# RWKV-7 branch beside sparse attention on one core: the RWKV step laid out anew, attention loads issued a unit ahead

## The chip, the cores and the metric

One core of a Trainium2 chip. Its engines each work through a queue of their own: TensorE (PE; PEld is its weight loads), VectorE (DVE), ScalarE (ACT), GpSimd (POOL) and SyncE (SP), whose queue issues the DMA transfers. The metric is the device time of one execution in microseconds, the median of the runs. PEclk in the profile is the TensorE clock that was granted, as a share of its upper level of 2.4 GHz; its lower level is 1.2 GHz.

## The reference

One layer over 2048 tokens, width 1024, all in float32: RMS norm, a projection into everything that follows, two branches, an output projection with residual, a final norm.

- **RWKV branch**, 8 heads of 64. Per token, state S (64x64 a head): `S = S*w_t + (S·(-kk_t))(kk_t*a_t)^T + v_t k_t^T`, `y_t = S r_t`. Then group norm over the 64 of each head, the bonus `sum(r*k*r_k)*v`, and a gate.
- **Sparse attention branch**, 8 heads: an index score per pair of query and key selects the 256 best keys of a query; softmax attention over those alone; an up-projection per head; a gate.

```
S   = S * w_t + sa * (kk_t * a_t) + v_t * k_t        # sa = S @ (-kk_t), 2048 steps
y_t = S @ r_t
y   = groupnorm(y) * gn_g + gn_b + sum(r * k * r_k) * v
out = rmsnorm(x + concat(y_rwkv * silu(g), o_attn * silu(g2)) @ w_out)
```

## The kernel before, in words

Four phases follow one another in the program text, and share the engines where their data allow. `phase_as` projects, builds the inputs of both branches in DRAM and the top-k masks (to about 986 us). `phase_r` is the RWKV branch, `phase_t` the attention, `phase_w` the output projection, whose first matmul is at 1917 us. RWKV and attention run side by side from 986 to 1917 us.

**RWKV.** The 2048 tokens are cut into 16 chunks of 128, a chunk into two halves (o = 0, 1) of 64 tokens. A chunk has two units (i = 0, 1), each with four of the eight heads. A unit is prepared (`prep`): one load `ld` of its five inputs (L938, two buffers), the running sum of the log decays by a scan on DVE (L951), exponentials on ACT, products into BK and X, and the products of all pairs of tokens on PE (L975) which DVE masks into E (L978). The bonus goes over `ld` once more: products on DVE, a matmul with ones (L983), times v (L985). `systems` sends the diagonal 32x32 blocks of E through DRAM (`du`, L1016) into the table A (L1018, one buffer). `inverse` inverts them on POOL: 31 steps of a multiplication (L1032) and an addition (L1034), each on the one before; the result goes out to `dx` (L1035) and comes back as the table TT (L1039). `prep2` transposes BK and v. `chain` is the recurrence of one half: reads of the state (L1052, L1059), a solve with TT on the first 32 tokens and on the other 32 (L1068), the new state (L1093, added on DVE at L1096), the outputs y. `tail` is the norm of a finished chunk's y, with a power on POOL in the middle (`rpow`, L130), then transposes of y on PE (L1115), scale, bonus, gate and store. In round n of the main loop: both units of chunk n+2 are prepared, chunk n+1 is inverted and transposed, the diagonal blocks of n+2 are sent, chunk n-1 gets its tail, and then both halves of the chain of chunk n run. All but the chain is traced under `later()`.

**Attention.** 64 units (p, b): four pairs of heads, 16 blocks of 128 queries. `scores` takes up to four matrices of 512 keys: two matmuls (L1240, L1241, a split into a high and a low part), evacuated with mask and running maximum by DVE into `sc`, `mx` (L1242), then the exponential on ACT. `attend` of the unit before transposes the weights (L1274), multiplies by v (L1283), gates with `ga` (L1296) and stores (L1297). The two take turns, 512 keys at a time. A unit's mask (L1224), queries (L1217), keys (L1205), values (L1207) and gates (L1265) are loaded by the unit itself when it comes to them.

**What sets the order.** A scheduler places every instruction in the queue of its engine by a planned time, taking the ready one of the highest priority; `later()` lowers the priority of what it encloses by one step, and all of attention stands two steps lower, so that it fills what RWKV leaves free. `issue_after(x)` makes what it encloses queue behind x on x's engine alone; it waits for nothing. Within a queue an instruction that waits holds all that stand behind it.

Of the kernel before, what the change touches and what calls it, by code (L numbers as in the profile page):

```python
# [7 lines left out]
F32 = mybir.dt.float32  # L8
# [10 lines left out]
T = 2048  # L19
# [868 lines left out]
def phase_r(env):  # L888
# [5 lines left out]
    C = 64  # L894
# [37 lines left out]
    def prep(tq, i, eC):  # L932
# [23 lines left out]
        G.tensor_copy(u.eC, eL[:, :, C])  # L956
# [3 lines left out]
        G.tensor_tensor(bp, kk, a, op=OP.mult)  # L960
# [5 lines left out]
        G.tensor_tensor(bp, bp, L, op=OP.mult)  # L966
# [55 lines left out]
    def inverse(A):  # L1022
# [7 lines left out]
        for s in range(31):  # L1030
            m, w = s // 4 + 1, 31 - s
            G.tensor_tensor(tmp[:, :m, :w], Xr[:, :m, s:s + 1].to_broadcast([128, m, w]),  # L1032
                            A[:, s:s + 1, s + 1:].to_broadcast([128, m, w]), op=OP.mult)
            G.tensor_tensor(Xr[:, :m, s + 1:], Xr[:, :m, s + 1:], tmp[:, :m, :w], op=OP.add)  # L1034
# [5 lines left out]
        return TT  # L1040

    def chain(us, TT, eC, y, n, o):
# [5 lines left out]
        def read(plane, pr):  # L1048
# [46 lines left out]
        for h in range(2):  # L1095
            V.tensor_tensor(S1[HALF[h], :, :, h], pS[HALF[h]], SP[HALF[h]], op=OP.add)  # L1096
        S.activation(y[:, o::2], read(1, pst([128, 2, 128], "rp", 2)), AF.Copy)

    def tail(us, y):
# [11 lines left out]
        rpow(st[:, 2], st[:, 1])  # L1111
        V.tensor_tensor(yv, yv, bc(st[:, 2]), op=OP.mult)
        pt = pst([128, NC, 2, C], "ch", 1)
# [19 lines left out]
    def prepare(n):  # L1133

        if n >= N:
            return None
        eC = tl([128, 2, NC], F32, "eC", 4)
        us = [prep(n, i, eC) for i in range(2)]
        return NS(dict(us=us, eC=eC))

    def prepare2(b, after=None):

        if b is None:
            return
        with tc.issue_after(after) if after else ExitStack():
            b.TT = inverse(b.A)
        for u in b.us:
            prep2(u)

    with e.later():  # L1150
        batch = {0: prepare(0)}
        batch[0].A = systems(batch[0].us)
        batch[1] = prepare(1)
        prepare2(batch[0])
        batch[1].A = systems(batch[1].us)
    tails = []
    for n in range(N):
        b = batch.pop(n)
        with e.later():
            batch[n + 2] = prepare(n + 2)  # L1160
            nx = batch.get(n + 1)
            prepare2(nx, batch[n + 2].us[1].last if batch[n + 2] else None)
            if batch[n + 2]:
                batch[n + 2].A = systems(batch[n + 2].us)
            if tails:
                tail(*tails.pop())
        y = tl([128, NC, 128], F32, "y", 2)
        for o in range(2):
            chain(b.us, b.TT, b.eC, y, n, o)
        tails.append((b.us, y))  # L1170
    with e.later():
        tail(*tails.pop())


def phase_t(env):
# [21 lines left out]
    KT, VT, Q = {}, {}, {}  # L1197

    def chunk_in(p, c):
# [10 lines left out]
    def queries_in(p, c):  # L1210

        Q[p, c] = []
        for i in range(2):
            q = tl([128, 2, 256], F32R, f"q{i}", 2)
            for h in range(2):
                for s in range(2):
                    dma(f32(q)[HALF[s], h], e.d_q[i][HALF[h], p, c * 256:c * 256 + 256])  # L1217
            Q[p, c].append(q)

    def scores(p, b, out):  # L1220

        n = (b + 1) * 128
        mk = tl([128, T], BF16, "mk", 3)
        dma(mk[:, :n], e.d_mask[b])  # L1224
        if b % 2 == 0:
            queries_in(p, b // 2)
# [5 lines left out]
        for nt, c0 in enumerate(range(0, n, C)):  # L1232
            w = min(C, n - c0)
            wp = max(w, 256)
            if (p, nt) not in KT:
                chunk_in(p, nt)
# [15 lines left out]
    def attend(p, b, rows, sums):  # L1252
# [11 lines left out]
        ga = tl([128, 128], F32, "ga", 3)  # L1264
        dma(ga, e.d_ga[p][:, ts])  # L1265
# [31 lines left out]
        dma(e.d_y[:, 4 + p, ts], ga)  # L1297

    units = [(p, b) for p in range(NP) for b in range(NB)]
    last = None  # L1300
    for u in units + [None]:
        out = []
        parts = [scores(*u, out)] if u else []
# [4 lines left out]
        last = (*u, *out) if u else None  # L1308

# [74 lines left out]
```

## Time and profile before

| | |
|---|---|
| median of 3 runs | 2110.79 us (2103.02, 2110.79, 2117.44) |
| the profiled execution | 2117.66 us, its span 2115.9 us |
| mean granted clock | 0.906 |
| busy: PE, DVE, ACT, POOL | 1815.5, 1290.4, 1018.7, 866.3 us |

The rows below are of that one execution. Times are in us from the span's start; Lnnn is a line of the kernel before. In a wait, the name behind the arrow is the instruction or transfer that came last of those waited for. A busy time is the sum over the instructions of an engine, so that a stretch less its busy time is idle.

### The profile page before, as it was taken

What the parts mean: (1) busy time and instruction counts of PE and PEld (TensorE: products, weight loads), DVE (VectorE), ACT (ScalarE), POOL (GpSimd) and SP (SyncE); (2) the same over time, 40 slices, a digit from 0 to 9 for tenths busy, and PEclk for the clock granted to TensorE, in tenths of its full rate; (3) what the DMA queues carried; (4) which work ended last, traced back from release to release, by engine and by line L of the source; (5) the groups of instructions that cost most, each with busy time, mean ns of one, the idle gap of its engine ahead of it and who ended that gap; (6) DMA issues with size and microseconds to landing.
All of it is one profiled execution on the core that took longest, in us unless ns stands there. A gap on an engine that the chain in (4) does not pass through costs nothing.

```text
span 2115.9 us, 36553 instructions
## 1 busy us (share of the span) xinstructions
PE 1815.5 (86%) x12906; PEld 1442.2 (68%) x12906; DVE 1290.4 (61%) x2986; ACT 1018.7 (48%) x1934; POOL 866.3 (41%) x2052
## 2 busy tenths in 40 slices
PE   5788998879796989896888877898889888978998
PEld 4666877658575867675667665777677766756886
DVE  5532538979788788986745555555656466524332
ACT  4422495453534754331355554556565655653321
POOL 1110224352545355553545445535655556441100
PEclk9778999989798999997589998999999999988999
DMA  7536334332262434224554354434543543224443
GB/s 247 197 100 202 98 105 135 105 108 88 69 236 63 137 119 140 80 92 132 148 140 111 105 150 112 113 84 111 151 116 100 143 135 103 75 62 165 130 145 111
DMA packets 311602, 262.53 MB, mean 124 GB/s; under 512 B 85105, under 2 KB 260849, under 8 KB 310257
## 3 DMA queue, kind: packets, MB, share of 16 engines
q1 hardware_dynamic: 307024, 248.04, 39.2%
q0 software_dynamic: 4384, 12.06, 1.8%
q8 instruction: 104, 1.70, 0.3%
q14 instruction: 90, 0.73, 0.1%
HBM read 166.37 MB, written 97.85 MB: 125 GB/s over the span
## 4 chain that ended last, share of the span: by engine, by line
PE 35%; DMA 10%; DVE 6%; POOL 4%; issue 2%; ACT 2%; SPq 1%; POOLq 0%; DVEq 0%; ACTq 0%
PE om L1283 5%; DMA ld<-d_rw 5%; PE tr L1274 5%; PE s L1240 3%; PE po L1345 3%; PE po L1346 3%; PE po L1348 3%; PE s L1241 2%; PE rp L975 2%; DMA dx<-Xr 2%; PE ch L1068 1%; DMA q<-d_q 1%; PE ch L1052 1%; PE rp L1059 1%; PE ch L1093 1%
## 5 line engine op out<-in xcount | busy, mean ns | idle before, releaser
L578 PE MATMUL pm<-xh,wh 128*128 128x512 f32 x800 | 330.4, 414 | 19.9 <-DVE t L589 11.8
L579 PE MATMUL pm<-xl,wh 128*128 128x512 f32 x800 | 328.0, 410 | 0.0
L580 PE MATMUL pm<-xh,wl 128*128 128x512 f32 x800 | 326.6, 408 | 0.0
L1242 DVE CUSTOM_DVE_ANT_0 sc<-s,mk 128x512 f32<-128x512 f32 (+3 forms) x320 | 187.5, 606 | 111.1 <-PE s L1241 62.4
L1276 ACT ACTIVATE pt<-tr 128x512 f32<-128x512 f32 (+1 forms) x288 | 157.5, 570 | 107.9 <-PE tr L1274 69.5
L578 PEld LDWEIGHTS pm<-xh,wh 128*128 128x128 f32 x800 | 158.4, 198 | 61.3 <-DVE t L589 13.7
L1240 PE MATMUL s<-kt,q 128*128 128x512 f32 (+2 forms) x320 | 149.7, 470 | 45.1 <-DVE mx L1242 29.3
L580 PEld LDWEIGHTS pm<-xh,wl 128*128 128x128 f32 x800 | 158.0, 197 | 36.3
L579 PEld LDWEIGHTS pm<-xl,wh 128*128 128x128 f32 x800 | 158.0, 198 | 35.5
L1274 PE MATMUL tr<-ident,sc 128*128 128x128 f32 x1088 | 179.1, 291 | 1.0 <-ACT pt L1276 0.9
L1249 ACT ACTIVATE sc<-sc,mx 128x128 f32<-128x128 f32 (+15 forms) x128 | 153.1, 1198 | 43.5 <-DVE mx L1248 42.8
L1283 PE MATMUL om<-pt,vt 128*64 128x128 f32 x2176 | 168.3, 290 | 0.8 <-DVE ga L1266 0.8
L1034 POOL TENSOR_TENSOR Xr<-Xr,Xtmp 128x60 f32<-128x60 f32 (+24 forms) x496 | 151.4, 305 | 34.2
L1032 POOL TENSOR_TENSOR Xtmp<-Xr,A 128x60 f32<-128x60 f32 (+24 forms) x496 | 146.5, 295 | 43.0 <-DMA A<-du 8.7
L1274 PEld LDWEIGHTS tr<-ident,sc 128*128 128x128 f32 x1088 | 132.9, 148 | 30.2 <-issue 12.5
L1283 PEld LDWEIGHTS om<-pt,vt 128*64 128x64 f32 x2176 | 129.9, 143 | 29.6 <-issue 15.6
L318 ACT ACTIVATE mk<-x,st 128x1920 bf16<-128x1920 f16 (+5 forms) x72 | 98.0, 1361 | 103.3 <-POOL st L315 103.3
L250 ACT ACTIVATE rl<-lg,wi 128x512 f32<-128x512 f32 (+3 forms) x152 | 93.9, 631 | 100.6 <-PE lg L248 51.8
L1241 PE MATMUL s<-kt,q 128*128 128x512 f32 (+2 forms) x320 | 125.5, 394 | 8.6 <-DMA q<-d_q 8.5
L321 DVE TENSOR_SCALAR_CACHE_REDUCE mk<-x,st 128x2048 bf16<-128x2048 f16 (+5 forms) x72 | 120.6, 1675 | 1.4
L1240 PEld LDWEIGHTS s<-kt,q 128*128 128x128 f32 x320 | 65.0, 203 | 70.2 <-DVE mx L1242 35.2
L255 DVE SCALAR_TENSOR_TENSOR xs<-rl,wi,xs 128x512 f32<-128x512 f32 (+3 forms) x108 | 73.5, 680 | 60.8 <-ACT rl L250 60.0
(329 smaller groups left out, 3975.1 us busy)
## 6 DMA issues: line engine op xcount, KB each, us to landing
wraw<-in_w_in_dram SPq DMA_DIRECT2D x42, 512.0 KB
d_rw<-t SPq DMA_DIRECT2D x80, 256.0 KB
ld<-d_rw SPq DMA_DIRECT2D x32, 640.0 KB
q<-d_q SPq DMA_DIRECT2D x256, 64.0 KB
d_q<-t SPq DMA_DIRECT2D x32, 256.0 KB
d_kt<-t SPq DMA_DIRECT2D x32, 256.0 KB
kt<-d_kt SPq DMA_DIRECT2D x64, 128.0 KB
A<-du SPq DMA_DIRECT2D x16, 512.0 KB
```

What stands on the lines that cost most here:

```text
L578: PE.matmul(pm, wh[:, k], XH[g][:, k], start=k == 0, stop=False)
L579: PE.matmul(pm, wh[:, k], XL[g][:, k], start=False, stop=False)
L580: PE.matmul(pm, wl[:, k], XH[g][:, k], start=False, stop=k == KD - 1)
L1032: G.tensor_tensor(tmp[:, :m, :w], Xr[:, :m, s:s + 1].to_broadcast([128, m, w]), A[:, s:s + 1, s + 1:].to_broadcast([128, m, w]), op=OP.mult)
L1034: G.tensor_tensor(Xr[:, :m, s + 1:], Xr[:, :m, s + 1:], tmp[:, :m, :w], op=OP.add)
L1240: PE.matmul(pS[:, :wp], qh[:, h, qs], k[:, h, :wp], start=True, stop=False)
L1241: PE.matmul(pS[:, :wp], ql[:, h, qs], k[:, h, :wp], start=False, stop=True)
L1242: V.tensor_tensor_reduce(out=rows[h][:, c0:c0 + w], in0=pS[:, :w], in1=mk[:, c0:c0 + w], scale=1.0, scalar=LOW, op0=OP.add, op1=OP.max, ac ...
L1249: S.activation(rows[h][:, :n], rows[h][:, :n], AF.Exp, bias=mx[:, h, 4:5], accum_out=sums[:, h:h + 1])
L1274: PE.transpose(pt[:, i, h], rows[h][:, (kb + i) * 128:(kb + i) * 128 + 128], ident)
L1276: S.activation(w[:, :m], pt[:, :m], AF.Copy)
L1283: PE.matmul(po[HALF[h]], v[:, (kb + i) % 4, HALF[h]], w[:, i, h], start=kb + i == 0, stop=kb + i == b)
```

## The change

The diff's first part is in `prep` and what it feeds. Two multiplications of a unit (`bp`) go from POOL to DVE, the copy of `eC` from POOL to ACT. The scaling of BK by eC queues on POOL behind an instruction that is handed in: the last step of an inverse. SV is no longer zeroed; the matmuls that read its missing half in the first read now contract over 64 rows instead of 128. `tail` becomes `tail_norm` and `tail_out`, `chain` returns its state addition on DVE, `inverse` its last step.

The main loop is written anew. Round n: the norm of chunk n-1, its power on POOL; the inverse of chunk n+1, queued on POOL behind that power; unit 0 of chunk n+2, its DVE rows queued behind the state addition of the half before; the chain's first half; the transposes and output of chunk n-1; `prep2` of chunk n+1; unit 1 of chunk n+2, queued behind the first half's state addition; the diagonal blocks of n+2; the chain's second half.

In attention `load` issues everything a unit needs, the gates too (`ga` has 5 buffers, before 3), one unit ahead of its scores; a store is issued behind the loads of a later unit; two DMA issues for the two heads of a key or query tile become one.

```
 prep:
-        G.tensor_copy(u.eC, eL[:, :, C])
+        S.activation(u.eC, eL[:, :, C], AF.Copy)
-        G.tensor_tensor(bp, kk, a, op=OP.mult)
+        V.tensor_tensor(bp, kk, a, op=OP.mult)
-        G.tensor_tensor(bp, bp, L, op=OP.mult)
+        V.tensor_tensor(bp, bp, L, op=OP.mult)
-        u.last = G.tensor_tensor(bk, bk, u.eC[:, :, None].to_broadcast([128, NC, 2 * C]), op=OP.mult).ins
+        with tc.issue_after(scaled_after):
+            G.tensor_tensor(bk, bk, u.eC[:, :, None].to_broadcast([128, NC, 2 * C]), op=OP.mult)
 prep2:
-        G.memset(u.SV[HALF[u.i]], 0.0)
 chain, read:
-                m = PE.matmul(pr[HALF[i], g, HALF[h]], us[i].E[:, h, 2 * g + o, plane * C:plane * C + C],
-                              us[i].SV[:, 2 * g + o, HALF[h]], start=False, stop=True, skip_group_check=True)
+                rows = slice(0, 128) if plane else HALF[1 - i]
+                m = PE.matmul(pr[HALF[i], g, HALF[h]], us[i].E[rows, h, 2 * g + o, plane * C:plane * C + C],
+                              us[i].SV[rows, 2 * g + o, HALF[h]], start=False, stop=True, skip_group_check=True)
 main loop (the old one is in the listing above):
+    batch = {}
+    first = G.memset(eLs[0][:, :, 0:1], 1.0).ins
     with e.later():
+        for n in range(2):
+            batch[n] = b = begin(n)
+            for i in range(2):
+                b.us.append(prep(n, i, b.eC, first))
+            b.A = systems(b.us)
+            if n == 0:
+                b.TT, first = inverse(b.A)
+                for u in b.us:
+                    prep2(u)
+    y0, b0, state = None, None, None
     for n in range(N):
         b = batch.pop(n)
+        new = batch[n + 2] = begin(n + 2) if n + 2 < N else None
+        nx = batch.get(n + 1)
+        norm = None
         with e.later():
+            if b0:
+                norm = tail_norm(y0)
+            if nx:
+                with behind(norm):
+                    nx.TT, first = inverse(nx.A)
+            if new:
+                with behind(state):
+                    new.us.append(prep(n + 2, 0, new.eC, first))
         y = tl([128, NC, 128], F32, "y", 2)
+        state = chain(b.us, b.TT, b.eC, y, n, 0)
+        with e.later():
+            if b0:
+                tail_out(b0.us, y0)
+            if nx:
+                for u in nx.us:
+                    prep2(u)
+            if new:
+                with behind(state):
+                    new.us.append(prep(n + 2, 1, new.eC, first))
+                new.A = systems(new.us)
+        state = chain(b.us, b.TT, b.eC, y, n, 1)
+        y0, b0 = y, b
 phase_t:
-        for h in range(2):
-            for i in range(2):
-                dma(f32(k)[HALF[i], h], e.d_kt[i][HALF[h], p, cs])
+        for i in range(2):
+            dma(f32(k)[HALF[i]], e.d_kt[i][:, p, cs].rearrange("(h d) t -> d h t", h=2))
...
+    def load(p, b):
+
+        if b % 4 == 0:
+            chunk_in(p, b // 4)
+        if b % 2 == 0:
+            queries_in(p, b // 2)
+        mk = MK[p, b] = tl([128, T], BF16, "mk", 3)
+        dma(mk[:, :(b + 1) * 128], e.d_mask[b])
+        ga = GA[p, b] = tl([128, 128], F32, "ga", 5)
+        return dma(ga, e.d_ga[p][:, b * 128:b * 128 + 128]).ins
...
-        dma(e.d_y[:, 4 + p, ts], ga)
+        stores.append((e.d_y[:, 4 + p, ts], ga))
...
+    load(*units[0])
+    for i, u in enumerate(units + [None]):
         out = []
+        ready, stores = stores, []
+        if i + 1 < len(units):
+            with tc.issue_after(load(*units[i + 1])):
+                for x in ready:
+                    dma(*x)
```

**What moves in the queues.** DVE's queue before, with the scan of a unit (L951, on `ld_1844`) a few rows behind the last masking of the unit before (L978, E_1806); L1242 evacuates scores, L1112 is the norm's last product:

```order
L1110 TENSOR_SCALAR gst_1825_10828<-gst_1825_10828 128x8
L951 SCALAR_TENSOR_TENSOR L_1846_11011<-restart_1341_7748,ld_1844_11007 128x256
L963 TENSOR_SCALAR ka_1849_11019<-ld_1844_11007,kac_247,oka_249 128x128 x2
L978 TENSOR_TENSOR E_1806_10695<-rp_1808_10697,mask_1342_7751 128x512
L1296 TENSOR_TENSOR ga_3067_16978<-ga_3067_16978,om_3068_16985 128x128
L1256 RECIPROCAL sums_3091_17054<-sums_3091_17054 128x2
L1242 ISA sc_3106_17112,mx_3108_17114<-s_3118_17143,mk_3103_17100 128x128
L1242 ISA mx_3108_17114 128x1
L1242 ISA sc_3107_17113,mx_3108_17114<-s_3119_17147,mk_3103_17100 128x128
```

And now, at a like place of a chunk: L1097 is the state addition (L1096 before), L1264 evacuates scores (L1242 before), L1287 and L1105 are rows of attention's gates and of the norm.

```order
L1097 TENSOR_TENSOR S0_1344_7769<-ch_1841_10964,SP_1840_10931 64x4x64 x2
L951 SCALAR_TENSOR_TENSOR L_1852_11080<-restart_1341_7748,ld_1850_11076 128x256
L960 TENSOR_TENSOR BK_1854_11086<-ld_1850_11076 128x4x64
L963 TENSOR_SCALAR ka_1855_11088<-ld_1850_11076,kac_247,oka_249 128x128 x2
L1287 TENSOR_TENSOR ga_2899_16179<-ga_2899_16179,om_2971_16457 128x128
L1081 TENSOR_TENSOR SP_1864_11132<-S0_1344_7769,eC_1733_10249 64x256 x2
L1105 TENSOR_REDUCE gst_1844_10990<-y_1806_10746 128x8
L1264 ISA sc_2964_16441,mx_2966_16443<-s_2986_16516,mk_2930_16306 128x384
L1264 ISA mx_2966_16443 128x1
```

The scan stood among rows of attention and of the norm, with the masking of the unit before behind it; now it stands right behind a state addition, and the unit's other rows behind it.

POOL's queue before, in an inverse (L1032, L1034 on Xr_2174), with the power of a norm (L130, `gst`) at the place that it has there:

```order
L1032 TENSOR_TENSOR Xtmp_2175_13245<-Xr_2174_13239,A_2154_13054 128x6x11
L1034 TENSOR_TENSOR Xr_2174_13239<-Xr_2174_13239,Xtmp_2175_13245 128x6x11
L1032 TENSOR_TENSOR Xtmp_2175_13245<-Xr_2174_13239,A_2154_13054 128x6x10
L1034 TENSOR_TENSOR Xr_2174_13239<-Xr_2174_13239,Xtmp_2175_13245 128x6x10
L130 TENSOR_TENSOR gst_2185_13344<-gst_2185_13344,mhalf_108 128x8
L1032 TENSOR_TENSOR Xtmp_2175_13245<-Xr_2174_13239,A_2154_13054 128x6x9
L1034 TENSOR_TENSOR Xr_2174_13239<-Xr_2174_13239,Xtmp_2175_13245 128x6x9
```

And now the end of one inverse and the beginning of the next; L988 is the scaling of BK (L987 before), L1113 the power:

```order
L1032 TENSOR_TENSOR Xtmp_2123_12857<-Xr_2122_12851,A_2112_12760 128x8
L1034 TENSOR_TENSOR Xr_2122_12851<-Xr_2122_12851,Xtmp_2123_12857 128x8
L988 TENSOR_TENSOR BK_2129_12936<-BK_2129_12936,eC_2118_12839 128x512
L988 TENSOR_TENSOR BK_2159_13099<-BK_2159_13099,eC_2118_12839 128x512
L1113 TENSOR_TENSOR gst_2173_13209<-gst_2173_13209,mhalf_108 128x8
L1026 MEMSET Xr_2176_13220 128x256
L1028 MEMSET Xr_2176_13220 32x8 x4
L1032 TENSOR_TENSOR Xtmp_2177_13226<-Xr_2176_13220,A_2167_13130 128x31
L1034 TENSOR_TENSOR Xr_2176_13220<-Xr_2176_13220,Xtmp_2177_13226 128x31
```

The power stood between two steps of the inverse; now it is ahead of the inverse's first row, behind the two scalings.

SP's queue before, around the table A (L1018), dx (L1035), TT (L1039) and the load `ld` (L938); L1297 stores attention's output, L1265 loads gates, L1224 a mask, L1016 sends diagonal blocks:

```order
L1297 DMA d_y_93<-ga_3565_18871 128x128
L1265 DMA ga_3635_19136<-d_ga_62 128x128
L1018 DMA A_2044_12310<-du_2043_12309 128x1x1024
L1035 DMA dx_2031_12203<-Xr_2032_12204 4x256x32
L1297 DMA d_y_93<-ga_3585_18945 128x128
L1224 DMA mk_3679_19327<-d_mask11_82 128x1536
L1039 DMA TT_2034_12274<-dx_2031_12203 32x8x32 x4
L938 DMA ld_2119_12867<-d_rw_63 128x10x128
L1016 DMA du_2098_12681<-E_2070_12515 32x8x32 x2
```

And now the same transfers (L1329 is the store, L1245 the gates, L1243 the mask):

```order
L938 DMA ld_1990_11979<-d_rw_63 128x10x128
L1016 DMA du_1946_11649<-E_1941_11629 32x8x32 x2
L1329 DMA d_y_93<-ga_3063_16851 128x128
L1245 DMA ga_3151_17136<-d_ga_62 128x128
L1018 DMA A_1947_11650<-du_1946_11649 128x1x1024
L1035 DMA dx_1901_11370<-Xr_1902_11371 4x256x32
L1243 DMA mk_3196_17300<-d_mask9_80 128x1280
L1329 DMA d_y_93<-ga_3077_16891 128x128
L1039 DMA TT_1904_11441<-dx_1901_11370 32x8x32 x4
L1245 DMA ga_3175_17221<-d_ga_62 128x128
L1016 DMA du_2001_12019<-E_1966_11836 32x8x32 x2
L938 DMA ld_2015_12186<-d_rw_63 128x10x128
```

The load stood behind TT; now the one load stands ahead of A, dx and TT, the other behind them. A still goes out just ahead of dx, and a store between dx and TT.

## Rows read from the trace of the kernel before

**Rows 1.** Page, part 1: engines' busy time, share of span, instructions.

```profile
PE 1815.5 (86%) x12906; PEld 1442.2 (68%) x12906; DVE 1290.4 (61%) x2986; ACT 1018.7 (48%) x1934; POOL 866.3 (41%) x2052
```

**Rows 2.** Stretches: span, length, busy us of each engine (instructions), clock, DMA share, GB/s.

```profile
986.00:1100.00 114.00, 89.84 (x585) 67.00 (x585) 68.67 (x207) 42.79 (x106) 58.50 (x158) 0.67 0.55 146
1100.00:1895.00 795.00, 691.82 (x7566) 547.91 (x7566) 440.50 (x1400) 457.74 (x996) 414.49 (x1142) 0.92 0.42 112
1895.00:1918.00 23.00, 8.85 (x152) 7.20 (x147) 14.01 (x21) 13.32 (x19) 0.00 (x0) 0.63 0.87 299
1918.00:2116.00 198.00, 187.58 (x992) 152.51 (x991) 68.00 (x80) 48.43 (x104) 25.22 (x58) 0.97 0.38 122
```

**Rows 3.** Waits of PE, 1100 to 1895 us: total us, times, longest us.

```profile
PE ch L1115 <- DVE y L1112: 35.6, 6, 9.8
PE s L1240 <- DVE mx L1242: 27.3, 9, 7.4
PE rp L983 <- DVE E L978: 22.3, 5, 9.0
PE s L1241 <- DMA q<-d_q: 8.3, 3, 6.6
```

**Rows 4.** Waits of DVE, the same stretch.

```profile
DVE L L951 <- DMA ld<-d_rw: 78.2, 12, 10.5
...
DVE ka L963 <- DMA ld<-d_rw: 24.2, 11, 5.9
```

**Rows 5.** Timeline of PE: start us, length us, [idle before, its releaser].

```profile
1639.14 0.70 PE L983 MATMUL rp<-ld,hsum 128*128 128x256 f32 x2
...
1651.01 0.79 PE L1240 MATMUL s<-kt,q 128*128 128x512 f32 x1 [5.18 <-DVE mx L1242]
```

**Rows 6.** Timeline of DVE, same piece.

```profile
1649.16 0.69 DVE L951 TENSOR_TENSOR_SCAN L<-restart,ld 128x256 f32<-128x256 f32 x1 [7.43 <-DMA ld<-d_rw]
```

**Rows 7.** Timeline of SP's queue, same piece.

```profile
1628.82 0.56 SPq L1018 DMA_DIRECT2D A<-du  x1
1629.48 0.55 SPq L1035 DMA_DIRECT2D dx<-Xr  x1
1631.72 7.58 SPq L1297 DMA_DIRECT2D d_y<-ga  x1
1641.24 2.84 SPq L1039 DMA_DIRECT2D TT<-dx  x4
...
1644.67 0.57 SPq L938 DMA_DIRECT2D ld<-d_rw  x1
```

**Rows 8.** Stretch behind the wait of rows 5, columns as in rows 2.

```profile
1650.00:1660.00 10.00, 8.99 (x38) 7.05 (x39) 6.49 (x21) 3.09 (x7) 4.03 (x11) 0.56 0.33 92
```

**Rows 9.** Timeline of DVE near 1878 us.

```profile
1878.36 0.77 DVE L1112 TENSOR_TENSOR y<-y,gst 128x512 f32<-128x512 f32 x1 [10.76 <-POOL gst L130]
```

**Rows 10.** Waits of PE, 986 to 1100 us.

```profile
PE s L1240 <- DMA q<-d_q: 11.1, 2, 8.5
```

**Rows 11.** Lines, 1100 to 1895: count | busy us, mean ns | idle before.

```profile
L1034 POOL TENSOR_TENSOR Xr<-Xr,Xtmp 128x60 f32<-128x60 f32 (+24 forms) x438 | 133.7, 305 | 30.5
...
L960 POOL TENSOR_TENSOR BK<-ld 128x256 f32<-128x256 f32 x24 | 19.3, 805 | 21.4 <-PE rp L997 21.4
L965 DVE TENSOR_TENSOR BK<-ld,L 128x256 f32<-128x256 f32 x24 | 14.9, 622 | 14.1 <-PE rp L997 8.1 <-ACT L L954 4.0 <-PE tr L1274 1.2
```

**Rows 12.** Chain that ended last: start us, length us, what.

```profile
1108.18 12.37 DMA A<-du
```

**Rows 13.** Timelines of DVE and POOL at 1660 us.

```profile
1660.33 0.69 DVE L1112 TENSOR_TENSOR y<-y,gst 128x512 f32<-128x512 f32 x1
1660.23 0.24 POOL L1034 TENSOR_TENSOR Xr<-Xr,Xtmp 128x30 f32<-128x30 f32 x1
1660.55 0.57 POOL L1032 TENSOR_TENSOR Xtmp<-Xr,A 128x29 f32<-128x29 f32 x1
```

**Rows 14.** The same chain at the end of the shared stretch.

```profile
1899.93 9.85 DMA wl<-d_wo
```

More of the change, by code (lines that the diff above doesn't have):

```diff
@@ L930, in phase_r, with prep @@
     fl = lambda t: t.rearrange("p a b -> p (a b)")
-    def prep(tq, i, eC):
+    def prep(tq, i, eC, scaled_after):
         sl = slice(tq * W, tq * W + W)
@@ L1039, in inverse @@
                 dma(TT[Q[2 * i + k]], dx[i, k].rearrange("u s t -> s u t"))
-        return TT
+        return TT, m_.ins
     def chain(us, TT, eC, y, n, o):
@@ L1095, in chain, with tail_norm @@
         for h in range(2):
-            V.tensor_tensor(S1[HALF[h], :, :, h], pS[HALF[h]], SP[HALF[h]], op=OP.add)
+            m = V.tensor_tensor(S1[HALF[h], :, :, h], pS[HALF[h]], SP[HALF[h]], op=OP.add)
         S.activation(y[:, o::2], read(1, pst([128, 2, 128], "rp", 2)), AF.Copy)
-    def tail(us, y):
+        return m.ins
+    def tail_norm(y):
         yv = y.rearrange("t c (h i) -> t (c h) i", h=2)
@@ L1110, in tail, with tail_out @@
         V.tensor_scalar(st[:, 1], st[:, 1], 1.0 / 64, 64e-5, op0=OP.mult, op1=OP.add)
-        rpow(st[:, 2], st[:, 1])
+        m = G.tensor_tensor(st[:, 2], st[:, 1], e.mhalf[:, :NU], op=OP.pow)
         V.tensor_tensor(yv, yv, bc(st[:, 2]), op=OP.mult)
+        return m.ins
+    def tail_out(us, y):
         pt = pst([128, NC, 2, C], "ch", 1)
@@ L1131, in phase_r @@
     N = T // W
[L1133 to L1148, printed above, removed]
-    with e.later():
[L1151 to L1155, printed above, removed]
@@ L1156, in phase_r, with behind, begin @@
-    tails = []
+    def behind(ins):
+        return tc.issue_after(ins) if ins else ExitStack()
+    def begin(n):
+        return NS(dict(n=n, eC=tl([128, 2, NC], F32, "eC", 4), us=[]))
+    batch = {}
+    first = G.memset(eLs[0][:, :, 0:1], 1.0).ins
+    with e.later():
+        for n in range(2):
[7 more added lines that the diff above has]
+                    prep2(u)
@@ L1167, in phase_r @@
-        y = tl([128, NC, 128], F32, "y", 2)
-        for o in range(2):
-            chain(b.us, b.TT, b.eC, y, n, o)
-        tails.append((b.us, y))
+            if b0:
[6 more added lines that the diff above has]
+                    new.us.append(prep(n + 2, 0, new.eC, first))
+        y = tl([128, NC, 128], F32, "y", 2)
+        state = chain(b.us, b.TT, b.eC, y, n, 0)
@@ L1171, in phase_r @@
+        with e.later():
[10 more added lines that the diff above has]
+        y0, b0 = y, b
     with e.later():
-        tail(*tails.pop())
+        tail_norm(y0)
+        tail_out(b0.us, y0)
@@ L1195, in phase_t @@
     V.tensor_tensor(sel.rearrange("p (a b) -> p a b", a=2), sel0[:, 0], sel0[:, 1], op=OP.add)
-    KT, VT, Q = {}, {}, {}
+    KT, VT, Q, MK, GA = {}, {}, {}, {}, {}
     def chunk_in(p, c):
@@ L1214, in queries_in @@
             q = tl([128, 2, 256], F32R, f"q{i}", 2)
-            for h in range(2):
-                for s in range(2):
-                    dma(f32(q)[HALF[s], h], e.d_q[i][HALF[h], p, c * 256:c * 256 + 256])
+            for s in range(2):
+                dma(f32(q)[HALF[s]], e.d_q[i][:, p, c * 256:c * 256 + 256].rearrange("(h d) t -> d h t", h=2))
             Q[p, c].append(q)
+    def load(p, b):
[7 more added lines that the diff above has]
+        return dma(ga, e.d_ga[p][:, b * 128:b * 128 + 128]).ins
     def scores(p, b, out):
         n = (b + 1) * 128
[L1223 to L1226, printed above, removed]
+        mk = MK.pop((p, b))
         qs = slice(b % 2 * 128, b % 2 * 128 + 128)
@@ L1234, in scores @@
             wp = max(w, 256)
-            if (p, nt) not in KT:
-                chunk_in(p, nt)
             k = KT[p, nt]
@@ L1263, in attend @@
         PE.matmul(pf[:, 0], sel, rh, start=True, stop=True)
-        ga = tl([128, 128], F32, "ga", 3)
-        dma(ga, e.d_ga[p][:, ts])
+        ga = GA.pop((p, b))
         V.tensor_tensor(ga, ga, pf[:, 0], op=OP.mult)
@@ L1296, in attend @@
         V.tensor_tensor(ga, ga, po, op=OP.mult)
-        dma(e.d_y[:, 4 + p, ts], ga)
+        stores.append((e.d_y[:, 4 + p, ts], ga))
     units = [(p, b) for p in range(NP) for b in range(NB)]
-    last = None
-    for u in units + [None]:
+    last, stores = None, []
+    load(*units[0])
+    for i, u in enumerate(units + [None]):
         out = []
+        ready, stores = stores, []
[3 more added lines that the diff above has]
+                    dma(*x)
+        else:
+            for x in ready:
+                dma(*x)
         parts = [scores(*u, out)] if u else []
@@ L1308, in phase_t @@
         last = (*u, *out) if u else None
+    for x in stores:
+        dma(*x)
 def phase_w(env):
```

9 lines of the change are left out of this document (1 added, 8 removed).

## The prediction

> **What bounds the kernel now.** I read the page first. TensorE (PE) is the busiest engine, 86% of the span [rows 1]. The shares of the engines per stage then tell where there is something to win: up to 986 us the program is the same before and after, the last 198 us (output projection) are 95% matmul at clock 0.97, and between them lie 932 us in which the RWKV branch and the attention share the engines. There PE is busy for 90 of 114, 692 of 795 and 9 of 23 us, at a granted clock of 0.67, 0.92 and 0.63 of full [rows 2]. So at most about 140 us of idle time, and what the half clock costs behind it, can be won.
>
> The list of waits names the rows PE stands idle for: the output transposes behind y (35.6 us), scores behind mx (27.3), the bonus matmul behind E (22.3), scores behind a query load (8.3) [rows 3]. Three of the four are released by VectorE (DVE), which is 55% busy. DVE in turn waits 102 us for one transfer, the 640 KB load `ld` of the five RWKV inputs [rows 4]. The timeline shows how one is the other. At 1639.1 us PE runs L983, the last reader of a buffer of `ld`. SP's queue is then held by a store of attention that waits for its data (7.6 us), and by TT behind dx, and issues the load at 1644.7 [rows 7]. DVE reaches the scan of the next unit (L951) and stands 7.4 us [rows 6]; everything behind it on DVE stands too, the evacuation of finished scores included, and PE runs dry for 5.2 us [rows 5]. Behind the wait PE runs ten microseconds at a mean clock of 0.56, 1.2 GHz for most of it [rows 8]. The other waits of the three rows have the same picture, but for two of the six of L1115 (3.9 and 7.9 us): there the power on GpSimd (POOL) stood behind rows of the inverse, and DVE waited 10.8 us for it [rows 9].
>
> **The change, part by part.**
>
> *Preparation, one unit to a half chunk.* In the order of the built program, the rows on DVE between the last masking of a unit (L978) and the scan two units later, which needs the same `ld` buffer, number 15 in the median before, 55 now. DVE takes 795 us for 1400 instructions in that stretch [rows 2], 0.57 us each with its waits, so the load has some 31 us instead of 9. The longest wait was 10.5 us [rows 4], on top of the 9: 19 of 31. On SP the load now stands ahead of A, dx and TT instead of behind them. So I take 85% of 35.6 - 11.8 + 27.3 + 22.3 = 73.4 us: **-62** (-45 to -73). What is late next is the table TT; see below.
>
> *Power ahead of the inverse.* It holds in every chunk of the new order: **-12**. The inverse now queues behind the norm, which costs nothing unless y is late, and lies in the estimate for TT.
>
> *Attention loads a unit ahead, stores behind them, half as many issues.* The query waits are 8.3 us here and 11.1 in the first 114 us [rows 3, 10]: **-14** (0 to -19).
>
> *Clock.* Mean 0.92 over 795 us [rows 2] is 64 us of cycles lost. Some 60% of that falls on running matmuls (the rest lies in idle time): 38. As most of the waits go, **-32** (-15 to -38).
>
> *Work moved.* Two multiplications a unit go from POOL (0.8 us each) to DVE, where the like one, L965, takes 0.62 us [rows 11]: 64 x 0.62 = 40 us more on an engine with room. But now the whole preparation stands right behind the state addition on DVE: some 10 us of DVE rows, while PE's order offers 11 to 18 us of other matmuls before it needs their result. **+8** (0 to 30). The copy of eC on ScalarE (32 x about 0.2 us), the missing memset of SV and its matmuls over 64 rows are hidden under attention's work there, which is half busy; if not, 0.2 us a unit is 6 us in all.
>
> *The new tight place: TT.* A unit is now prepared much later, so the path from its masked products to the first solve has less cover. I counted the matmuls of the new order between the bonus matmul of a chunk's second unit and the chunk's first solve, each at its spacing at full clock in PE's timeline: 45 to 58 us, 53 in the mean, where before it was about 100. What must happen meanwhile: two maskings and two stores of E (about 2.5 us), their landing (2.5, as the shortest query loads on the chain), A (12.4 us, [rows 12]), the inverse, dx and TT. The inverse is 62 steps of 0.30 us [rows 11] and four gate multiplications, 22 us busy, and took 30 in the stretch of the rows with more company; say 25. From dx's issue to that of TT it is 11.8 us in the rows when A goes out just ahead [rows 7], 5 at best; TT's four issues take 2.8, and 2 for landing. Sum 51 to 58. Taking 54.5, and stretching the cover by 8% for the waits that remain, five of the fifteen chunks come short, by 24 us together: **+24** (0 to 100).
>
> The Trainium skill ("SBUF — State Buffer", section "Who interferes with whom") has a rule against this part: a VectorE operation with two SBUF inputs and a GpSimd one that reads SBUF exclude each other for the whole instruction. One step of the inverse beside such a DVE row took 0.57 us, its neighbour 0.24 [rows 13], as the rule has it. By the rule alone the 40 us would be added to the inverses, 2.5 us each, and the sum would end near 2075. I leave it out of the sum, because POOL is rid of the same multiplications, 1.6 us a unit, that stood among the steps of the inverse.
>
> *The end.* RWKV now finishes about eight units of attention before the end, and not inside the output projection. That moves matmuls and adds none. But the 23 us before the first output matmul, which wait for the output weights [rows 14] and in which PE found 9 us of RWKV work, will be empty: **+9** (0 to 9).
>
> Sum: -62 - 12 - 14 - 32 + 8 + 24 + 9 = -79. The profiled execution took 2117.7 us (span 2115.9), so 2039. The median of the runs is 6.9 lower; I take 3 for that and predict **2036**.
>
> **The rivals.**
>
> *A. The forecast*, 2000 to 2065: 0.56.
>
> *B. TT becomes the wait.* If every path takes 58 us, A ahead of dx each time, the shortfalls are 47 us and a third of the clock stays lost: 2036 + 23 + 10 = 2069, up to 2090. For it: A is issued just ahead of dx in about half the chunks of the new order. Against: PE never waited for TT before, and slack grows with any other wait. 0.16.
>
> *C. Slower.* The same path with SP held as in the rows: a store 7.6 us ahead of TT [rows 7], so 64 to 66 us. The shortfalls are then about 118 us, 94 more than in the sum, and half the clock is lost again: 2036 + 94 + 16 = 2146. It decides from a path of about 62 us on. Against: the order puts stores of a unit already finished, and behind loads. 0.08.
>
> *D. The waits for `ld` only move.* SP still issues it late, since its issue waits for the buffer and stands behind others. Then 62 + 32 us come back but for a quarter: near 2105. The new count of rows speaks against it. 0.12.
>
> *E. More*: no shortfall at TT, all waits gone, -73 - 12 - 19 - 38 + 9 = -133: 1985. 0.08.
>
> Between 2090 and 2131 lies what a measurement of this kernel can't tell from no change (1%). Faster: A, B, E, and nothing of D: 0.80. Same: D: 0.12. Slower: C: 0.08. The range of eight in ten leaves out C, most of D, and half of E: 1990 to 2095.
>
> **What would show it.** The row of DVE waiting for `ld` under 25 us (102 now); L1115 without a wait over 2 us; PE idle in the shared stretch about 60 to 75 us instead of 103, and its clock 0.95 or more; a new row "PE ch L1068 (now L1069) behind DMA TT" of 10 to 40 us: over 60 it is B, over 110 C. If DVE still waits 70 us for `ld`, D is right and my count of rows was no measure of time. Attention alone at the end should keep PE over 90% busy; if it doesn't, the sum misses a wait between PE, ScalarE and DVE that RWKV's matmuls filled.

## The result and the profile after

The changed kernel takes **2142.9 us** (median of 4 runs, 2141.9 to 2145.7) against 2112.7 us: 1.0129 times the time before, interval 1.0102 to 1.0156. That is slower, by 1.3%; 2036 was forecast, with 1990 to 2095 as the range. Only the rival C, at 0.08, ended where the time is.

The stretches of the profile after, with the columns of [rows 2]; the output projection now starts at 1957 us, before at 1918:

```profile
986.00:1100.00 114.00, 87.53 (x769) 66.46 (x766) 67.36 (x227) 51.02 (x130) 43.45 (x135) 0.82 0.66 154
1100.00:1895.00 795.00, 681.76 (x7338) 530.81 (x7338) 452.62 (x1393) 436.03 (x985) 374.07 (x1044) 0.88 0.42 109
1895.00:1957.00 62.00, 40.81 (x390) 31.01 (x389) 26.34 (x69) 37.53 (x57) 0.00 (x0) 0.87 0.29 101
1957.00:2144.00 187.00, 176.17 (x768) 145.41 (x768) 61.02 (x64) 39.44 (x80) 15.02 (x48) 0.97 0.39 130
```

In the same 795 us PE is idle for 113 us instead of 103, and its clock is 0.88 instead of 0.92. From 986 us to the first output matmul the stretch is 39 us longer (971 us, before 932): PE is idle for 161 us instead of 142, and the lower clock costs the running matmuls 88 us instead of 68 (half of the time in which the trace has the clock at its lower level and a matmul running). The waits of PE in the 795 us, which answer to [rows 3]:

```profile
PE ch L1069 <- DMA TT<-dx: 82.6, 14, 9.6
PE s L1262 <- DVE mx L1264: 12.3, 14, 2.4
PE om L1304 <- DVE ga L1287: 6.6, 7, 1.6
PE tr L1295 <- ACT pt L1297: 4.9, 6, 1.8
```

Every row of [rows 3] is gone or less than half: the transposes behind y, the bonus matmul behind E, the queries. One row has come: the chunk's first solve behind the table TT, 82.6 us here and 91.6 from 980 to 1950 us. DVE waits 5.7 us for `ld` in that longer stretch, in [rows 4] it was 102:

```profile
DVE L L951 <- DMA ld<-d_rw: 5.7, 3, 2.5
```

Of the signs that the prediction named, three came: this row is under 25 us, the output transposes (L1121 now) have no wait, and attention alone, once RWKV is done, keeps PE busy for 68.8 of the 73 us from 1865 to 1938, which is 94%. Idle time and clock did not come, and the row of TT, 82.6 us, lies where the sign says B (over 60, under 110), while the time is that of C.

What makes TT late can be read off two chunks. SP's queue at 1288 us:

```profile
1288.25 0.57 SPq L1018 DMA_DIRECT2D A<-du  x1
1288.91 0.56 SPq L1035 DMA_DIRECT2D dx<-Xr  x1
1301.00 1.81 SPq L1039 DMA_DIRECT2D TT<-dx  x4
```

and PE's first solve of that chunk, with its idle time in brackets:

```profile
1302.91 0.39 PE L1069 MATMUL ch<-R,TT 32*32 32x64 f32 x2 [9.64 <-DMA TT<-dx]
```

A, the 512 KB load of the *next* chunk, has just gone out when dx (128 KB) does, since both wait for the end of the inverse: dx for its result, A for its one buffer, which the inverse has read till then. TT cannot go out until dx has landed, 12.1 us on. So it is in 8 of the 14 chunks from the third on, with 11.1 to 12.1 us from dx to TT. In four others A goes out between dx and TT, as here in SP's queue at 1499 us:

```profile
1498.88 0.56 SPq L1035 DMA_DIRECT2D dx<-Xr  x1
1499.55 2.79 SPq L1018 DMA_DIRECT2D A<-du  x1
1504.41 1.81 SPq L1039 DMA_DIRECT2D TT<-dx  x4
```

and PE's solve behind it:

```profile
1513.86 1.38 PE L1069 MATMUL ch<-R,TT 32*32 32x64 f32 x16 [9.50 <-DMA TT<-dx]
```

Now dx lands after 5.5 us, but the solve that waits for TT comes 9.4 us after TT's first issue. Either way it is 14 to 15 us from dx to the solve. The inverse itself is also later and longer than it need be. POOL's timeline has the power ahead of it, waiting for DVE's part of the norm, and the output's bonus and gate (`yo`, an addition and a multiplication) between its steps, waiting for ACT:

```profile
1243.36 1.66 POOL L1113 TENSOR_TENSOR gst<-gst,mhalf 128x8 f32<-128x8 f32 x1 [4.62 <-DVE gst L1112]
...
1324.50 0.72 POOL L1129 TENSOR_TENSOR yo<-yo,bv 128x256 f32<-128x256 f32 x1 [14.41 <-ACT yo L1127]
```

### The profile page after: what moved, and what is told of

It is laid out like the page before. It is cut to its first block, busy times and chain, and to the rows that moved or that the text cites. A ratio compares the mean times of both kernels' runs of the same rounds, so it can differ in the third digit from the quotient of the medians.

```text
span 2144.0 us, 36181 instructions
## 1 busy us (share of the span) xinstructions
PE 1818.9 (85%) x12906; PEld 1435.7 (67%) x12906; DVE 1313.2 (61%) x3050; ACT 1022.5 (48%) x1966; POOL 800.7 (37%) x1925
## 4 chain that ended last, share of the span: by engine, by line
PE 26%; DMA 11%; POOL 9%; issue 7%; DVE 4%; ACT 2%; SPq 1%; POOLq 0%; DVEq 0%; ACTq 0%
DMA dx<-Xr 5%; PE tr L1295 4%; PE om L1304 3%; POOL Xr L1034 3%; POOL Xtmp L1032 3%; PE po L1377 3%; PE po L1378 3%; PE po L1380 3%; PE s L1262 2%; PE s L1263 2%; DMA TT<-dx 2%; PE ch L1069 1%; DMA q<-d_q 1%; PE rp L975 1%; DMA d_y<-ga 1%
## 5 line engine op out<-in xcount | busy, mean ns | idle before, releaser
L1264 DVE CUSTOM_DVE_ANT_0 sc<-s,mk 128x512 f32<-128x512 f32 (+3 forms) x320 | 188.7, 607 | 161.2 <-PE s L1263 127.6
L1297 ACT ACTIVATE pt<-tr 128x512 f32<-128x512 f32 (+1 forms) x288 | 158.4, 570 | 142.2 <-PE tr L1295 81.6
L1304 PE MATMUL om<-pt,vt 128*64 128x128 f32 x2176 | 172.8, 296 | 7.4 <-DVE ga L1287 7.3
L1032 POOL TENSOR_TENSOR Xtmp<-Xr,A 128x60 f32<-128x60 f32 (+24 forms) x496 | 148.6, 300 | 55.3 <-DMA A<-du 18.1
L1034 POOL TENSOR_TENSOR Xr<-Xr,Xtmp 128x60 f32<-128x60 f32 (+24 forms) x496 | 149.0, 300 | 37.1
L1304 PEld LDWEIGHTS om<-pt,vt 128*64 128x64 f32 x2176 | 134.8, 147 | 35.2 <-issue 17.0
L1069 PE MATMUL ch<-R,TT 32*32 32x64 f32 x1024 | 53.3, 242 | 92.0 <-DMA TT<-dx 91.6
L1377 PE MATMUL po<-wh,yh 128*128 128x512 f32 x256 | 100.9, 394 | 19.4 <-ACT yh L1368 19.4
```

The lines of the kernel that those rows point to most:

```text
L1034: m_ = G.tensor_tensor(Xr[:, :m, s + 1:], Xr[:, :m, s + 1:], tmp[:, :m, :w], op=OP.add)
L1264: V.tensor_tensor_reduce(out=rows[h][:, c0:c0 + w], in0=pS[:, :w], in1=mk[:, c0:c0 + w], scale=1.0, scalar=LOW, op0=OP.add, op1=OP.max, ac ...
L1297: S.activation(w[:, :m], pt[:, :m], AF.Copy)
L1304: PE.matmul(po[HALF[h]], v[:, (kb + i) % 4, HALF[h]], w[:, i, h], start=kb + i == 0, stop=kb + i == b)
L1377: PE.matmul(po, yh[:, m], wh[:, m, ds], start=m == 0, stop=False)
```

## The experiments

Each was timed against the kernel before on its own chip, so the ratios compare best. P is the theory that the path to TT is longer than its cover, which is the other matmuls that PE has until the chunk's first solve; the other letters are told in the expectations. "The gate" is short for queueing the inverse behind the norm's power.

**Which half of the change.** Attention's part alone, then RWKV's alone (`phase_r` of the one with `phase_t` of the other).

> Attention of the change with the RWKV branch of before. Theory P (the changed kernel is slow because the path from a chunk's masked products over A, the inverse, dx and TT, 60 to 78 us in its trace, is longer than the other matmuls that PE has until the chunk's first solve): the path keeps its old cover of over 100 us, no wait for TT; the query waits (19.6 us before) fall to about 10, nothing else moves: 2095 to 2115. Theory Q (the rival: attention's loads and stores in their new order hold SP's queue, 86 us behind stores in the changed trace against 52 before, and A, dx, TT and ld with it): 2125 to 2145, and DVE waits for ld over 130 us.

2085.7 us, 0.9860 (0.9825 to 0.9894). Not what Q says: attention's part is a gain of 28 us, more than its query waits, and more than P's range allows. The waits for `ld` stay, as they should.

> RWKV branch of the change with the attention of before. P: PE waits for TT 80 to 100 us as in the changed kernel, 2140 to 2155. Q: SP is as free as before, TT waits under 30 us, 2060 to 2110.

2152.2 us, 1.0165 (1.0123 to 1.0207), TT waits 91.5 us. The loss lies in the RWKV part; attention's new loads and stores show no share in it.

**The gate taken away, and more cover.**

```
-                with behind(norm):
-                    nx.TT, first = inverse(nx.A)
+                nx.TT, first = inverse(nx.A)
```

> The changed kernel, but the inverse isn't queued behind the norm's power: the power falls between steps of the inverse, as before. P with the gate as one of three lengths of the path (in 7 chunks the inverse starts 5 to 12 us after A has landed, right behind the power, 54 us together; the other two are the waits for yo inside the inverse, 70 us, and A just ahead of dx, 57 us): TT waits fall from 92 to 45 to 60 us, waits of L1121 behind y come back with 10 to 20 us: 2105 to 2130. If the gate costs nothing (my prediction's claim): 2140 to 2155, TT waits of 85 us or more.

2144.9 us, 1.0122 (1.0077 to 1.0166): no change, though TT waits fell to 28 us. DVE now stands for the power, which waits its turn among the steps of the inverse:

```profile
DVE y L1114 <- POOL gst L1113: 129.7, 12, 18.1
```

Both expectations missed: one wait took the other's place. Next, more cover (unit 1 and `systems` moved ahead of the first chain):

```
-                    new.us.append(prep(n + 2, 0, new.eC, first))
+                    for i in range(2):
+                        new.us.append(prep(n + 2, i, new.eC, first))
+                new.A = systems(new.us)
         y = tl([128, NC, 128], F32, "y", 2)
...                  # the same of unit 1, and systems, gone behind the first half
```

> The changed kernel, but both units of a chunk are prepared in the first half's slot, ahead of the first chain, and the diagonal blocks sent there: half a chunk (about 25 us) more cover for the path. P with the lost cover as cause: TT waits under 25 us, 2050 to 2095, unless the waits for ld come back (over 40 us). If the inverse's start is bound by the norm's power and not by A: TT waits stay over 60 us, 2115 to 2145.

2162.0 us, 1.0232 (1.0187 to 1.0276), TT waits 104 us. The second expectation had the cause, though its range ended at 2145. A lands early and is of no use, since the inverse follows the power at once, which had waited 25 us:

```profile
1496.89 1.74 POOL L1113 TENSOR_TENSOR gst<-gst,mhalf 128x8 f32<-128x8 f32 x1 [25.30 <-DMA mk<-d_mask]
1498.58 0.32 POOL L1026 MEMSET Xr<- 128x256 f32 x1
1498.96 0.53 POOL L1028 MEMSET Xr<- 32x8 f32 x4
1499.57 0.24 POOL L1032 TENSOR_TENSOR Xtmp<-Xr,A 128x31 f32<-128x31 f32 x1
```

**The power off POOL.**

```
-        m = G.tensor_tensor(st[:, 2], st[:, 1], e.mhalf[:, :NU], op=OP.pow)
+        S.activation(st[:, 2], st[:, 1], AF.Sqrt)
+        m = V.reciprocal(st[:, 2], st[:, 2])
...
-                with behind(norm):
-                    nx.TT, first = inverse(nx.A)
+                nx.TT, first = inverse(nx.A)
```

The gate goes with it here, as in every run below that has the power off POOL.

> The changed kernel with the norm's power taken off POOL (square root on ACT, reciprocal on DVE), so that norm and inverse no longer hold each other; the inverse starts when A is there. Theory N (norm and inverse now fall at the same time, and whichever is first on POOL holds the other: power first gave 92 us of TT waits, inverse first gave 130 us of DVE waiting for the power): DVE waits under 10 us for the norm, TT waits 15 to 40 us (path of 58 to 62 us as without the gate), 2060 to 2095. If the clash is not the cause and the late preparation alone is: TT waits over 60 us, 2110 to 2145.

2139.8 us, 1.0126 (1.0051 to 1.0200). TT waits 23 us, as N said, and the time did not move: N falls as the whole cause. The next one in POOL's queue holds DVE, `yo` behind the inverse, whose release of bv the next unit needs:

```profile
DVE bv L985 <- POOL yo L1130: 91.8, 13, 13.6
```

With both units together as well it was 2156.9 us, 1.0210 (1.0146 to 1.0275), where N had 2040 to 2080, and with `yo` moved on top of that:

> The changed kernel with both units prepared in the first half's slot, the power off POOL (square root on ACT, reciprocal on DVE) and yo on DVE. Without yo moved this was 2157 us: TT waits only 12 us, but 80 us of DVE waiting for bv, whose buffer yo on POOL still held behind the inverse. Theory H (several pieces of work of a round sit behind one another in the queues of POOL and SP, and each one that is taken out lets the next hold): TT waits under 20 us, no wait for bv, and 2080 to 2115 if SP has nothing that holds; 2120 to 2150 if SP's dx stands there for the inverse over 80 us, with du, A and attention's loads behind it, as in the run with all shortenings. Theory P (the path's length against its cover is all): 2050 to 2085.

2158.8 us, 1.0209 (1.0181 to 1.0237). No long wait for bv, TT 12 us, but dx stands at the head of SP's queue until the inverse is done, with all other loads behind it, as H has it; the time is above H's range, and whether this wait makes it, no run shows:

```profile
SPq L1035 <- POOL Xr L1034: 157.9, 14, 18.2
```

**yo off POOL** (`G.tensor_tensor(yo, ...)` to `V.tensor_tensor(yo, ...)`, twice).

> The changed kernel with the bonus and the gate of the output (yo) on DVE, so that nothing stands between the steps of the inverse; the power stays ahead of it. If the yo waits inside the inverse (70 us over 8 chunks) lie on the path: TT waits 45 to 70 us, 2105 to 2130. N alone: the inverse ends earlier, but every start still follows the power; half of it is lost there: 2120 to 2140.

2110.7 us, 0.9993 (0.9965 to 1.0021): 1.4% won, some 29 us, the power left where the change put it. TT waits are still 87 us, but the inverse takes 24 us instead of 31 in the mean, and a chunk 47 us instead of 50 from solve to solve.

> All shortenings of the path together: power off POOL, yo on DVE, and A's load issued behind TT instead of just ahead of dx (11 to 12 us from dx to TT in every second chunk of the changed kernel, 5 in the others). Path 48 to 56 us against 45 to 58 of other matmuls: TT waits under 15 us, 2040 to 2075. If DVE, which has yo too, becomes the bound: rows of PE behind mx, ga or y over 60 us, 2100 or more.

2147.1 us, 1.0157 (1.0095 to 1.0219): a miss. TT waits 46 us, and SP stands 139.5 us with dx at its head. My reading is that the inverse, with nothing on POOL to queue behind, is planned early, and dx queued ahead of work that could go.

**A behind TT**, the power left ahead of the inverse:

```
+        with behind(after):          # after: the last DMA of TT of the chunk before
             dma(A.rearrange("l s t -> l (s t)"), ...)
...
-                new.A = systems(new.us)
+                new.A = systems(new.us, tt)
```

> The changed kernel with yo on DVE and A's load queued behind TT; the power stays ahead of the inverse. With yo moved alone: 2111 us, TT waits 87 us, in 8 of 14 chunks 12 us from dx to TT. P: 6 to 7 us shorter there, A 5 us later where the inverse waits for the power anyway: TT waits 45 to 65 us, 2080 to 2100. H: A later makes the inverse of the other chunks late, the waits only change places: 2105 to 2135.

With `yo` on DVE too: **2050.3 us, 0.9727 (0.9674 to 0.9780)**, the fastest of the study, with two variants below that do not differ from it. The waits for TT, 46 us, are in P's range, the time is 30 us below it. SP's queue, where dx now lands after 4.7 us:

```profile
1173.03 0.56 SPq L1036 DMA_DIRECT2D dx<-Xr  x1
1177.73 1.79 SPq L1040 DMA_DIRECT2D TT<-dx  x4
1179.56 0.55 SPq L1019 DMA_DIRECT2D A<-du  x1
```

and the stretch from 1100 us to the end of RWKV, 642 us long, with PE idle for 47 of them:

```profile
1100.00:1742.00 642.00, 594.80 (x6966) 462.30 (x6962) 434.31 (x1361) 405.45 (x932) 333.84 (x980) 0.94 0.50 128
```

> The changed kernel with A's load queued behind TT and nothing else; yo stays on POOL inside the inverse. yo moved alone gave -32 us (2111), both together -93 (2050). If the two add up: 2075 to 2090. If yo's waits (the inverse then took 27 to 40 us) keep every chunk late however A goes: 2110 to 2135, and TT waits over 70 us.

2076.1 us, 0.9816 (0.9777 to 0.9855): A's place alone is worth 67 us. By the ratios that is 66, `yo` 29 and both together 85, so the two add up but for 10 us, which is within the intervals. From dx to TT it is 4.7 to 6.8 us in all chunks but the first. PE's waits for TT in 1100 to 1895 us, and POOL's for `yo`:

```profile
PE ch L1070 <- DMA TT<-dx: 31.2, 14, 7.0
POOL yo L1130 <- ACT yo L1128: 27.8, 4, 21.1
```

In the changed kernel the second row was

```profile
POOL yo L1129 <- ACT yo L1127: 85.4, 13, 14.4
```

It fell though `yo` stayed where it was, and POOL's waits ahead of the power fell from 227 to 169 us: with TT in time, y is in time.

> The 2050 us kernel (yo on DVE, A behind TT) with the inverse not queued behind the norm's power, which then falls between its steps. If the power ahead is what this layout needs: DVE waits over 80 us for the power as in the like run with yo on POOL (130 us), PE behind mx, y and the state addition: 2085 to 2130. If it only delays the inverse: TT waits under 25 us, 2020 to 2045.

2162.2 us, 1.0216 (1.0174 to 1.0257), above both ranges, and DVE stands 128.1 us behind the power. So the gate is what this layout needs, and its price is small beside that. The power between the steps is not the only reason: the run with the power off POOL, `yo` on DVE and A behind TT, which lacks the gate too, took 2147 us. All six runs without the gate took 2140 to 2162 us. In each of them POOL stands for 185 to 244 us of the 795 at the head of an inverse whose A has not landed, in the changed kernel never; here it is

```profile
POOL Xtmp L1033 <- DMA A<-du: 209.8, 14, 22.8
```

What waited behind it differed: the power, `yo`, or dx on SP.

> The 2050 us kernel with the attention of before: what attention's part of the change is worth there. In the old loop it was worth 28 us, in the changed one 9: 2055 to 2080. If SP, held by stores, makes TT late: 2080 to 2100, with TT waits over 70 us.

2063.1 us, 0.9738 (0.9709 to 0.9768): the interval overlaps that of the kernel with the new attention. The 28 us that the new one gave in the old loop are not there to be won here.

> The 2050 us kernel with A loaded in two pieces, the rows of the first 8 steps ahead of the others. In that kernel a chunk takes 43 us, which is what one round of A (10 to 13 us from issue to the inverse's start), inverse (24), dx to TT (5) and TT's issues (1.4) sums to, since A has one buffer and is issued behind TT. If that ring sets the pace: the inverse starts some 6 us earlier where the power is there, TT waits 10 to 30 us (46 now), 2010 to 2040. If the norm's power sets the start anyway: 2043 to 2055.

2056.3 us, 0.9712 (0.9680 to 0.9743), no different. The ring over A's buffer does not set the pace: the inverse starts right behind the power, which waits for the norm on DVE:

```profile
1454.42 1.65 POOL L1116 TENSOR_TENSOR gst<-gst,mhalf 128x8 f32<-128x8 f32 x1 [12.48 <-DVE gst L1115]
1456.02 0.32 POOL L1029 MEMSET Xr<- 128x256 f32 x1
1456.40 0.53 POOL L1031 MEMSET Xr<- 32x8 f32 x4
1457.01 0.24 POOL L1035 TENSOR_TENSOR Xtmp<-Xr,A 128x31 f32<-128x31 f32 x1
```

**Controls on A.** The same edit in the kernel before, and dx queued behind A in every chunk of the changed one.

> The kernel before with A's load queued behind TT. There, too, A goes out just ahead of dx in most chunks and TT is issued 11 to 13 us behind dx instead of 5, but the first solve comes 12 to 45 us after TT. If A's place costs only where the solve waits for TT: 2100 to 2125, no change. If A ahead of dx costs in itself (SP's queue, the DMA engines): 2070 to 2095.

2120.9 us, 1.0026 (1.0006 to 1.0045): no gain, a trace of a loss, though the edit did its work: from dx to TT it is 4.7 to 5.5 us in all sixteen chunks, where it was 10.8 to 13.6 in eleven. So A's place costs nothing in the old loop, where no solve waits for TT.

> The changed kernel with dx queued behind A in every chunk, where it was so in 8 of 14: 11 to 12 us from dx to TT throughout. If A's place is the largest part of the loss: TT waits 110 to 150 us, 2165 to 2200. If each chunk's loss is made up in the next (the chunks with 5 us had longer inverses): 2135 to 2160.

2163.6 us, 1.0215 (1.0188 to 1.0241), TT waits 107 us: between the two expectations. From dx to TT it was 10.3 to 12.9 us in all chunks but the last. It was no doubling: in four of the six chunks that I had counted as free of A, A had gone out between dx and TT and made TT's own landing late.

**The small edits**, with attention's part, in the old loop (`bp` on DVE, `eC` on ACT, SV's memset and rows), and then `yo` on DVE.

> Attention of the change and, in the main loop of before, the small edits of prep alone: bp on DVE, eC on ACT, SV without its memset and read over 64 rows. Prediction's term for them: 0 to +30 with +8 as the guess, so 2086 to 2116 against 2086 without them. Rival: POOL is freed of 1.6 us a unit that stands in the inverse, and of the memset that waits there: 2060 to 2085.

2107.4 us, 0.9968 (0.9945 to 0.9991), 1.1% above attention's part alone: 22 us, in the range of the term, above its guess.

> The kernel with the small edits and attention of the change in the main loop of before, and yo on DVE as well: POOL then holds inverse, power and scaling alone. If yo on POOL costs in the old loop as in the new one (32 us there): 2040 to 2075. If it is costly only where every chunk waits for its inverse: 2075 to 2100, since no solve waits for TT in the old loop.

2080.2 us, 0.9851 (0.9824 to 0.9878). In the second expectation's range, but `yo` gives 1.2%, 25 us, in the old loop too, where no solve waits for TT; why, no run here tells. So its 29 us in the changed loop need not come by way of TT either, whose waits fell by 5 us there.

## Why the prediction was wrong, step by step

- **Preparation a unit to a half chunk, -62, and the power, -12: right.** DVE's 102 us for `ld` are 6, and the three rows of PE behind them, 85 us with the power's 12, are 12. The two are 73 us together, 74 were forecast.
- **Query loads, -14**: the waits went from 19.4 to 11.8 us, 8 of 14. That the part gives 28 us in the old loop I did not foresee.
- **Work moved, +8 (0 to 30)**: 22 us in the old loop; in the changed one no run took it out.
- **The end, +9: right in kind.** PE stands 19.4 us ahead of the first output matmul, with nothing to do. Before, 14 of those 23 us were idle, so it is 5 more.
- **TT, +24: the step that failed.** The waits are 92 us. The path was put at 51 to 58 us from E to solve, 54.5 for the sum (its own terms add up to 52 to 59). Over chunks 2 to 15 the timelines have 60 to 78, 70 in the mean: 6.7 to A's issue (5 in the sum), 17.5 from there to the inverse (12.4), 31.3 for the inverse (25), 1.5 to dx's issue, 8.8 to TT's, 4.4 to the solve. Three things were mis-sized:
  - "The inverse now queues behind the norm, which costs nothing unless y is late": y is late as soon as TT is, and in 7 of the 14 chunks the inverse starts 19 to 26 us after A's issue, right behind the power.
  - `yo` wasn't looked at: its wait stood in 8 inverses for 4 to 14 us each. With `yo` on DVE the inverse takes 24 us, as the sum had it. In the kernel before it took 31 in the mean as well; the sum took 25 against the 30 that it had read.
  - A was counted as a toll of dx in half of the chunks, where it takes 6 to 7 us of either dx or TT in 12 of 14. [rows 7] and the order of the transfers show A just ahead of dx; the old loop paid the same toll unseen, under 12 to 45 us of slack between TT and the solve.
- **Shortfalls one by one.** I set each chunk's path against its cover. But norm, inverse, TT, solve and again the norm form a ring: a late solve makes the next power late. That fits what the runs show: with A's 6 to 7 us out, POOL's waits for the norm and for `yo` fell too, and the gain was 67 us. Between the two profiled executions it is 72: PE's idle time from 986 us to the first output matmul went from 161 to 111 us (TT's part from 91.6 to 42.8), and the clock's loss on running matmuls from 88 to 64. A chunk's pace alone is not the time: from solve to solve it took 57 us in the kernel before and 50 in the slower one.
- **Clock, -32: the wrong sign, and a miss nearly as large as that of TT.** At 0.92, 64 us of the 795 were lost [rows 2], at 0.88 it is 95; on running matmuls 36 (38 in the prediction) became 74. From 986 us to the first output matmul it is 68 against 88: +20, not -32. Waits did not go, they changed places: PE's idle spells of over 1.5 us in the 795 us are 16 with 89 us together before, 15 with 86 after. But the clock's spells at its lower level, 18 instead of 16, last 11.0 us in the mean instead of 7.5, three of them 20 to 31 us. Why they last longer, no run shows.
- **Rival C** had the right place and nearly the right time, 2146, and the right threshold (62 us), but not the mechanism, so that its time is luck. No store held TT: TT's issue waited for dx (59.3 us in 15 waits). The 7.6 us of the store in [rows 7], which the prediction took for a wait for its data, are the store's own issue, right behind A and dx; its data was there when it began. In the changed kernel a load of gates takes as long in the same place; from dx to TT it is 11.8 us there, and 12.1 where nothing stood between them. So C added to the path what the toll of A already held. The place deserved more than 0.08 all the same: the sum of the path had no allowance for a queue. The load of gates:

```profile
1445.76 0.55 SPq L1035 DMA_DIRECT2D dx<-Xr  x1
1446.40 9.17 SPq L1245 DMA_DIRECT2D ga<-d_ga  x1
1457.51 1.80 SPq L1039 DMA_DIRECT2D TT<-dx  x4
```

- **The rule of the Trainium skill** ("SBUF — State Buffer", section "Who interferes with whom") would have given 2075. The trace does not bear it out as the loss: the 62 steps of an inverse were busy for 17.5 to 19.9 us over the chunks from the third on, before for 17.7 to 19.2.

How A's place works on the path, the timelines of the run with A's place alone tell: 60 us in the mean instead of 70, with 6 less from dx to the solve, 7 less from A's issue to the inverse and 5 less in the inverse, against 8 more to A's issue, which now comes later. What stays open: why the clock's low spells are longer; why the runs without the gate all take 2140 to 2162 us, whichever wait they have; and why attention's part and `yo` give 28 and 25 us in the old loop, more than the waits that they remove.

## What to carry to other kernels

A table that each round needs sits at the end of a ring; when work is moved closer to its use, lay out the whole ring with every queue in it, the transfers of the *next* round too, before trusting the cover. Removing one wait of a ring proves little: three removals here (the gate, the power on POOL, and `yo` with both units together) moved the time by nothing, since another wait in the queues of POOL or SP took its place. And an instruction that two DMAs wait for together (here the inverse's last step, for A and dx) sends both out at once: queue the large one behind the urgent one. What that is worth depends on who waits: 67 us here, nothing in the loop where TT had slack.

## What the runs showed of the hardware

The 512 KB load A just ahead of the 128 KB store dx, in the same queue, delayed it by 6 to 7 us: from dx to TT it was 10.3 to 12.9 us with dx queued behind A, and 4.7 to 6.8 with A behind TT. Between dx and its reading back, A delayed the reading: 9 us from TT's issue to the solve instead of 2. And another transfer issued within 3 us of dx, with A ahead of both, held SP's queue in its own issue for 7 to 10 us, as the 9.17 us above. Whether this arises in the queue or in the DMA engines, no run tells; A and dx shared a queue in all.

After a wait of PE the clock could stay at its lower level for long while PE was fully busy: behind the wait that ended at 1302.9 us these 14 us have a clock of 0.52, in [rows 8] it was 0.56 over 10:

```profile
1306.00:1320.00 14.00, 14.00 (x126) 10.91 (x127) 5.32 (x16) 4.13 (x11) 3.24 (x11) 0.52 0.30 86
```
